# Gated tiles leave PSUM as copies and are split in the last product, and two waits and the opening are set anew, in a two-layer macaron trunk

## The chip, the core and the metric

One Trainium2 chip, one core. The metric is the device time of one execution in microseconds; the kernel before has a median of 2362.59 us over 3 runs (2360.82 to 2363.31).

The engines have their usual short names: PE is TensorE, ACT is ScalarE, DVE is VectorE, POOL is GpSimd and SP is SyncE. A name such as L189 is line 189 of the kernel before. In the changed kernel the lines below the first edit have moved down by up to seven, so L1284 there is L1291, and L915 is L921.

## The reference

The input is one sequence of 512 tokens by 1024 features, and a memory of 256 tokens by 1024. There are two layers; each is a half step of a gated feed-forward net, a mixing step of three gated attention branches, and another half step.

```python
def _swiglu(t, w_gate, w_up, w_down):
    return (jax.nn.silu(t @ w_gate) * (t @ w_up)) @ w_down

for l in range(DEPTH):                                  # DEPTH = 2
    f = _swiglu(_rmsnorm(h, ffn1_pre_g[l]), ffn1_w_gate[l], ffn1_w_up[l], ffn1_w_down[l])
    h = h + 0.5 * _rmsnorm(f, ffn1_post_g[l])
    u = _rmsnorm(h, mix_pre_g[l])
    proj = u @ w_in[l]                                  # q, k, v of two branches, q of the memory branch, forget logits
    o_sb = _stick_breaking_attention(...)               # 8 heads of 64
    o_fx = _forgetting_attention(...)                   # 8 heads of 64
    o_mem = _memory_attention(...)                      # 4 heads of 128
    merged = (g_sb * (_merge_heads(o_sb) @ w_br_sb[l])
              + g_fx * (_merge_heads(o_fx) @ w_br_fox[l])
              + g_mem * (_merge_heads(o_mem) @ w_br_mem[l]))
    h = h + _rmsnorm(merged @ w_out[l], mix_post_g[l])
    f = _swiglu(_rmsnorm(h, ffn2_pre_g[l]), ffn2_w_gate[l], ffn2_w_up[l], ffn2_w_down[l])
    h = h + 0.5 * _rmsnorm(f, ffn2_post_g[l])
```

The hidden width of the feed-forward net is 2816, which is 22 tiles of 128.

## The kernel before

**Products in three passes.** Every factor is kept as two rounded halves, a high and a low one. `split` (L183 to L201) makes them: ACT copies the source into the high half (L188; L191 with a scale), DVE subtracts the high half from the source (L189; L192 with a scale). `mm3` (L214, L215, L216) then issues three matmuls: high by high, high by low, low by high. So each weight tile and each activation needs one ACT copy and one DVE subtraction before PE can finish with it.

**Feed-forward nets.** There are four: a0 and c0 in the first layer, a1 and c1 in the second. Gate and up products run in five groups of four hidden tiles (0, 4, 8, 12 and 16) and two hidden tiles, 20 and 21, that run early. Within a group the product is a block algorithm with seven block products, numbered 0 to 6. ACT and DVE turn the results into the gated tiles, named `ca` in the nets a and `cc` in the nets c. `feature_major` (L777) has PE transpose them into PSUM (tiles `tha`, `thc`). Groups 0 to 12 leave PSUM as plain ACT copies into the `hr` tiles. The last group, 16, leaves PSUM already split, half by half, into the tiles `hid16` and `hid18` (h and l): per net four ACT copies and four DVE subtractions of 128x512.

**The down products.** They are the same block algorithm in 14 steps (`product`), seven products of two halves each, in the order 0, 2, 3, 4, 5, 1, 6. The weights are the `wh_da`/`wl_da` tiles and their sources `bta` and `raw_da`. The other factor is `aa` (`ac` in the nets c): `first_factor` forms a sum or a difference of `hr` tiles into `asa` (L915, L917), and splits it into `aa` by an ACT copy and a DVE subtraction. Hidden tiles 16 to 21 are left out of the block algorithm; `down` multiplies them plainly afterwards, and that is where `hid16` and `hid18` are read. `feature_major` for the last group stands in the schedule beside products 0 and 2.

**Heads.** A stick-breaking head (`stick_head`) computes its scores `zs`, runs a chain of ACT and DVE operations that ends in `ts` (L1315), has PE transpose `ts` block by block into `pts` (`transposed`, L1284), splits those, and multiplies by the values (`pvs`, L1271). A forgetting head does the same with `zf`, `pf` (L1355) and `ptf`. Head (p, j) is head j of pair p.

**What sets the order.** `Q` holds a list of matrix products (gate products `pg`, branch products `pb`, query and key products `pq`, `pk`). `Q.weave` runs a head's chain beside them: a chain step `("wait", t)` says that t us of products are to be issued ahead of the next step. The waits of the stick-breaking heads are `W_SB0` and `W_SB1` plus an entry of the table `W_MORE` (L1414). The framework's scheduler may still issue a single instruction earlier where its own estimate sees PE without work. ACT and DVE serve products and chains from one queue each, in that order.

**The opening.** `begin` (L1715 on) normalises the four 128-token tiles of x; `scaled` writes one half (512 features) of a tile, `turn` transposes it on PE and has ACT copy it out (`us_x`). ACT and DVE run in the written order here (`in_order`). Tiles 2 and 3 are transposed later by `turned` (L613), each behind a wait in us of products.

Of the kernel before, what the change touches and what calls it, by code (L numbers as in the profile page):

```python
# [9 lines left out]
F32 = mybir.dt.float32  # L10
# [7 lines left out]
P = 128  # L18
# [4 lines left out]
def kernel(  # L23
# [38 lines left out]
    nc = tc.nc  # L62
    _, S, D = x.shape
# [41 lines left out]
    def stile(shape, tag, name, dt=F32R):  # L105
        return sb.tile(shape, dt, tag=tag, bufs=BUFS[tag], name=name)
# [4 lines left out]
    def pbank(tag, name):  # L111
        return ps.tile([P, S], F32, tag=tag, bufs=4, name=name)
# [69 lines left out]
    HALVES = (slice(0, S // 2), slice(S // 2, S))  # L182
    FULL = slice(0, S)  # L183

    def split(h_ap, l_ap, src, scale=None, later=False):

        if scale is None:
            both = [nc.scalar.copy(h_ap, src)]  # L188
            make = lambda: nc.vector.tensor_tensor(l_ap, src, h_ap.bitcast(F32), ALU.subtract)  # L189
        else:  # L190
            both = [nc.scalar.activation(h_ap, src, AF.Copy, scale=scale)]  # L191
            make = lambda: nc.vector.scalar_tensor_tensor(l_ap, src, scale, h_ap.bitcast(F32), ALU.mult, ALU.subtract)  # L192
        if later:
            return make
        both.append(make())
        if Q.pinned:
            for ins in both:
                tc.keep_in_program_order(ins)
# [164 lines left out]
    def wpair(src, ktiles, c0, name, scale=None):  # L363

        return [Unit(src, k, min(4, ktiles - k), c0, 256, f"{name}_{k}", scale) for k in range(0, ktiles, 4)]
# [110 lines left out]
    Q = Queue()  # L476
# [8 lines left out]
    def new_h(name):  # L485

        hT[:] = [stile([P, D], "o", f"h{name}_{t}", F32) for t in range(NT)]
# [4 lines left out]
    def rstd(st, a, b=None, pre=None):  # L492

        s, m, y, w = st[:, a:a + 1], st[:, 3:4], st[:, 4:5], st[:, 5:6]
        if pre is not None:
            nc.scalar.activation(y, s, AF.Ln, bias=st[:, pre:pre + 1])
            nc.vector.tensor_scalar(m, s, st[:, pre:pre + 1], None, ALU.add)  # L500
        elif b is None:
            nc.scalar.activation(y, s, AF.Ln, bias=eps_t[:])
            nc.vector.tensor_scalar(m, s, D * EPS, None, ALU.add)
        else:
            nc.vector.tensor_scalar(m, s, st[:, b:b + 1], D * EPS, ALU.add, ALU.add)
            nc.scalar.activation(y, m, AF.Ln)
        nc.scalar.activation(y, y, AF.Exp, scale=-0.5)

        nc.vector.scalar_tensor_tensor(w, m, y, y, ALU.mult, ALU.mult)
        nc.vector.scalar_tensor_tensor(y, w, -3.0, y, ALU.add, ALU.mult)  # L510
        return y

    class Sub:
# [17 lines left out]
        def begin(self):  # L531
            self.fs = [stile([P, D], "f", f"f{self.name}_{t}", F32) for t in range(NT)]
# [100 lines left out]
    TG = (0, 4, 8, 12, 16)  # L633
# [6 lines left out]
    def ffn(l, src, wg, wu, wd, dst, name, spare, aside=None):  # L640
# [5 lines left out]
        hid, st = {}, {}  # L646
        hr = {}
# [14 lines left out]
        def pair(f):  # L662

            i = f // 2
            if i not in hr:
                hr[i] = stile([P, 2, S], HR[i], f"hr{name}_{i}", F32)
            return hr[i]
# [108 lines left out]
        def feature_major(f, of=(0, 1)):  # L776

            for i in of:
                u = st.pop(("hid", f, i))
                for b in range(2):  # L780
                    f2 = f + 2 * b
                    pt = pbank("z", f"th{name}_{f2}_{i}")
                    for m in range(2):
                        for e in range(2):
                            nc.tensor.transpose(pt[:, (2 * m + e) * P:(2 * m + e + 1) * P],
                                                u[:, e, (2 * b + m) * P:(2 * b + m + 1) * P], ident[:])
                    yield 0.45
                    out_ = pt[:].rearrange("p (m q) -> p m q", m=2)
                    if f2 < NC * FC:
                        nc.scalar.copy(pair(f2)[:, :, HALVES[i]], out_)  # L790
                        continue
                    if i == 0:
                        st["hl", b] = [stile([P, 2, S], "v", f"hid{name}_{f2}{x}") for x in "hl"]
                        for m in range(2):
                            hid[f2 + m] = tuple(t[:, m] for t in st["hl", b])
                    split(*(t[:, :, HALVES[i]] for t in st["hl", b]), out_)

        def block_units(order, keep, rows, nm, src, pair=None, c0=0):

# [181 lines left out]
        later = []  # L981
# [6 lines left out]
        def some(n):  # L988
            for one in itertools.islice(todo, n):
                Q.add(*one)  # L990
# [10 lines left out]
        ug, uu = (wpair(w[l], ND, EARLY * P, f"{x}{name}_{EARLY}") for x, w in (("g", wg), ("u", wu)))  # L1001
# [43 lines left out]
        if aside is not None:  # L1045
            Q.add([], lambda: iter((next(norm),)))
            Q.add([], lambda: iter((next(norm),)))
        some(1)
        if aside is not None:
            Q.add([], lambda: norm)  # L1050
# [315 lines left out]
    def mem_head(q, ks, vs, hd, ot, name, begun):  # L1366
# [37 lines left out]
        for kt in range(MT):  # L1404
# [6 lines left out]
    W_SB0, W_SB1 = 12.0, 4.7  # L1411


    W_MORE = {(0, 0): (-8.0, -1.5), (0, 1): (-0.7, -1.0), (1, 0): (0.8, 0.0), (1, 1): (0.5, -1.3),  # L1414
              (2, 0): (-1.0, 0.0), (2, 1): (-0.5, 1.5), (NP - 1, 0): (0.0, 2.5), (NP - 1, 1): (1.0, 0.0)}
    W_FX0, W_FX1 = 6.0, 4.2
    W_MM0, W_MM1 = 6.0, 4.5
# [28 lines left out]
    def mixing(l, src, ks, vs, values, dst):  # L1446
# [187 lines left out]
        def run():  # L1634
# [32 lines left out]
            def stick(p, j):  # L1667
                return stick_head(st["q", 0, p], st["k", 0, p], lambda kt: st["v", 0][kt][:, p], j, st["o", 0][p], f"s{l}_{p}_{j}",
                                  W_MORE.get((p, j), (0.0, 0.0)))

# [43 lines left out]
    def warm(n):  # L1714

        for _ in range(n):
            tc.keep_in_program_order(nc.tensor.matmul(wps[:], wsb[:, 0:P], wsb[:, 0:S], start=True, stop=True))

    def begin():

        sub = subs[0]
        new_h("x")
        Q.hold = True
        nc.sync.dma_start(hT[0][:], x[0, 0:P, :])
        warm(6)
        sub.gains(quick=True)
        nc.sync.dma_start(hT[1][:], x[0, P:2 * P, :])

        ug = Q.jobs[0][0][:4]
        for un in ug[2:]:  # L1730
            un.place = "v"
        for un in ug[:2]:
            un.fetch()
        nc.sync.dma_start(hT[2][:], x[0, 2 * P:3 * P, :])
        for un in ug[2:]:
            un.fetch()
        nc.sync.dma_start(hT[3][:], x[0, 3 * P:4 * P, :])
        sub.begin()
        sub.alloc()
        lows = {}  # L1740

        def turn(t, hf):
            ts_ = slice(t * P, (t + 1) * P)
            pt = pbank("z", f"utx_{t}_{hf}")
            for e in range(4):
                d = 4 * hf + e
                nc.tensor.transpose(pt[:, e * P:(e + 1) * P], sub.fs[t][:, d * P:(d + 1) * P], ident[:])
            lows[t, hf] = split(sub.us[hf][:, :, 0, ts_], sub.us[hf][:, :, 1, ts_],
                                pt[:].rearrange("p (e q) -> p e q", e=4), scale=RS, later=True)

        def stats(t):
            sub.squared(hT[t][:], sub.sh[t], 0, sub.fs[t][:])
            return rstd(sub.sh[t], 0)

        def scaled(t, hf, r):
            nc.vector.scalar_tensor_tensor(sub.fs[t][:, HF[hf]], hT[t][:, HF[hf]], r, sub.spread[hf][:], ALU.mult, ALU.mult)

        with in_order(nc.scalar, nc.vector):
            r = stats(0)
            for hf in range(2):  # L1760
                scaled(0, hf, r)
            r = stats(1)
            warm(2)
            for hf in range(2):
                turn(0, hf)
            low0 = ug[0].split_from(ug[0].raw[:], later=True)
            for hf in range(2):
                scaled(1, hf, r)
            turn(1, 0)
            turn(1, 1)  # L1770
            low1 = ug[1].split_from(ug[1].raw[:], later=True)
            lows[0, 0]()
            lows[1, 0]()
            low0()
            ug[0].loaded()
            lows[0, 1]()
            lows[1, 1]()
            low1()
            ug[1].loaded()
            r = stats(2)  # L1780
            for hf in range(2):
                scaled(2, hf, r)
            for un in ug[2:]:
                un.load()
            for pt, c in zip(sub.spread, HF):
                nc.scalar.copy(sub.gq[:, c], pt[:])
            sub.squared(hT[3][:], sub.sh[3], 0, sub.fs[3][:])
            sub.normed(3)
        sub.done.update((0, 1))
        for t, us_ in ((2, 6.5), (3, 3.2)):  # L1790
            yield ("wait", us_)
            sub.turned(t)
            yield ("pe", 0.9)
# [9 lines left out]
    for l in LAYERS:  # L1803
        i, mn = 3 * l, []
# [42 lines left out]
```

## Time and profile before

| what | value |
|---|---|
| median of 3 runs | 2362.59 us |
| profiled execution, its own time | 2360.91 us |
| its span, first to last instruction | 2359.2 us |
| DVE busy | 1781.2 us (75%) |
| ACT busy | 1445.6 us (61%) |
| POOL busy | 212.5 us (9%) |
| mean granted TensorE clock | 1.000 |

The span is the stretch from the first to the last instruction. The profiled execution's own time is 1.7 us longer, which is what lies around the span, and it is itself 1.7 us below the median of the runs. In a row of the view in order of time stand the start, the length, the engine, the line, the operation with its output and inputs, and the count; a bracket gives the idle time of the engine before the row and what ended it. Matmuls overlap, so the time that a wait costs PE is read from start to start.

### The profile page before, as it was taken

How to read it: one execution, taken by the hardware profiler on the slowest of the kernel's cores; microseconds unless marked ns; L12 is line 12 of the kernel's file. 1: busy time of each engine (PE TensorE's matmuls, PEld its weight loads, DVE VectorE, ACT ScalarE, POOL GpSimd, SP SyncE). 2: the span in 40 equal slices, each digit the busy share in tenths (PEclk: the TensorE clock that was granted, in tenths of full speed). 3: DMA queues.
4: the chain of work that ended last, by engine and by line, in shares of the span. 5: the costliest groups of instructions: out<-in, count | busy, mean ns of one | idle time of the engine just before them, and what ended most of it. 6: DMA issues, size and time to landing. Idle time of an engine off the chain costs nothing.

```text
span 2359.2 us, 30541 instructions
## 1 busy us (share of the span) xinstructions
PE 2346.2 (99%) x11368; PEld 1970.5 (84%) x11368; DVE 1781.2 (75%) x2431; ACT 1445.6 (61%) x2339; POOL 212.5 (9%) x242
## 2 busy tenths in 40 slices
PE   9999999999999999999999999999999999999998
PEld 8888888888888888888888888888888888888887
DVE  8766977678776687769887679766787766866696
ACT  6665665577665565566665566656675555655574
POOL 1101100001020011101011110000011100111100
PEclk9999999999999999999999999999999999999999
DMA  8866854222223476659586767632232234776683
GB/s 246 233 181 173 222 186 144 72 72 81 82 71 116 152 217 175 180 159 245 180 217 172 186 187 222 196 101 81 63 90 81 72 123 154 222 184 173 182 219 99
DMA packets 233112, 366.46 MB, mean 155 GB/s; under 512 B 11242, under 2 KB 101634, under 8 KB 232452
## 3 DMA queue, kind: packets, MB, share of 16 engines
q1 hardware_dynamic: 202400, 305.76, 40.2%
q0 software_dynamic: 30560, 58.76, 14.5%
q8 instruction: 89, 1.46, 0.3%
q14 instruction: 59, 0.48, 0.1%
q10 hardware_dynamic: 4, 0.00, 0.0%
HBM read 349.80 MB, written 14.68 MB: 154 GB/s over the span
## 4 chain that ended last, share of the span: by engine, by line
PE 92%; DVE 5%; issue 1%; ACT 1%; DMA 1%; POOL 0%; SPq 0%; DVEq 0%; POOLq 0%
PE ptc L214 5%; PE ptc L216 5%; PE ptc L215 5%; PE pta L214 5%; PE pta L215 5%; PE pta L216 5%; PE pg L216 3%; PE pg L214 3%; PE pg L215 3%; PE pdc L216 3%; PE pda L216 3%; PE pdc L214 3%; PE pdc L215 3%; PE pda L215 3%; PE pda L214 3%; PE pb L214 2%
## 5 line engine op out<-in xcount | busy, mean ns | idle before, releaser
L214 PE MATMUL pg<-us_a,wh_wg 128*128 128x512 f32 x384 | 151.0, 393 | 0.0
L216 PE MATMUL pg<-us_a,wl_wg 128*128 128x512 f32 x384 | 149.8, 390 | 0.0
L215 PE MATMUL pg<-us_a,wh_wg 128*128 128x512 f32 x384 | 149.7, 390 | 0.0
L189 DVE TENSOR_TENSOR wl_tc<-ktc,wh_tc 128x1024 fp32r<-128x1024 f32 x80 | 97.7, 1224 | 63.3 <-ACT wh_tc L188 63.1
L189 DVE TENSOR_TENSOR wl_ta<-kta,wh_ta 128x1024 fp32r<-128x1024 f32 x80 | 97.7, 1224 | 57.5 <-ACT wh_ta L188 57.5
L188 ACT CAST wh_tc<-ktc 128x1024 fp32r<-128x1024 f32 x80 | 84.0, 1053 | 67.9 <-PE ptc L216 48.0
L214 PE MATMUL pta<-wh_ta,aga 128*128 128x512 f32 x320 | 125.3, 392 | 0.0
L214 PE MATMUL ptc<-wh_tc,agc 128*128 128x512 f32 x320 | 125.3, 393 | 0.0
L216 PE MATMUL pta<-wh_ta,aga 128*128 128x512 f32 x320 | 124.8, 390 | 0.3 <-DVE aga L189 0.3
L216 PE MATMUL ptc<-wh_tc,agc 128*128 128x512 f32 x320 | 124.7, 390 | 0.0
L215 PE MATMUL ptc<-wl_tc,agc 128*128 128x512 f32 x320 | 124.7, 390 | 0.0
L215 PE MATMUL pta<-wl_ta,aga 128*128 128x512 f32 x320 | 124.7, 390 | 0.0
L188 ACT CAST wh_ta<-kta 128x1024 fp32r<-128x1024 f32 x80 | 84.0, 1053 | 65.1 <-PE pta L216 43.6
L189 DVE TENSOR_TENSOR wl_tc<-raw_tc,wh_tc 128x1024 fp32r<-128x1024 f32 x56 | 68.6, 1225 | 45.3 <-ACT wh_tc L188 45.3
L189 DVE TENSOR_TENSOR wl_ta<-raw_ta,wh_ta 128x1024 fp32r<-128x1024 f32 x58 | 70.9, 1224 | 42.2 <-ACT wh_ta L188 42.2
L188 ACT CAST wh_tc<-raw_tc 128x1024 fp32r<-128x1024 f32 x56 | 58.9, 1052 | 48.2 <-PE ptc L216 36.6
L188 ACT CAST wh_ta<-raw_ta 128x1024 fp32r<-128x1024 f32 x58 | 60.8, 1050 | 44.9 <-PE pta L216 37.0
L216 PE MATMUL pdc<-wh_dc,ac 128*128 128x512 f32 x224 | 87.5, 392 | 0.7 <-DVE ac L189 0.7
L216 PE MATMUL pda<-wh_da,aa 128*128 128x512 f32 x224 | 87.4, 392 | 0.7 <-DVE aa L189 0.7
L214 PE MATMUL ptc<-wh_tc,us_b 128*128 128x512 f32 x224 | 87.7, 392 | 0.2
L214 PE MATMUL pda<-wh_da,aa 128*128 128x512 f32 x224 | 87.6, 391 | 0.0
L214 PE MATMUL pdc<-wh_dc,ac 128*128 128x512 f32 x224 | 87.6, 391 | 0.0
(557 smaller groups left out, 7409.8 us busy)
## 6 DMA issues: line engine op xcount, KB each, us to landing
raw_wg<-in_w_gate_dram SPq DMA_DIRECT2D x48, 512.0 KB, 3.7
raw_ta<-in_ffn_w_gate_dram SPq DMA_DIRECT2D x44, 512.0 KB, 4.3
raw_tc<-in_ffn_w_gate_dram SPq DMA_DIRECT2D x44, 512.0 KB, 4.3
raw_da<-in_ffn_w_down_dram SPq DMA_DIRECT2D x42, 512.0 KB, 3.8
raw_dc<-in_ffn_w_down_dram SPq DMA_DIRECT2D x42, 512.0 KB, 3.8
kta<-in_ffn_w_up_dram SPq DMA_DIRECT2D x40, 512.0 KB, 6.5
ktc<-in_ffn_w_up_dram SPq DMA_DIRECT2D x40, 512.0 KB, 5.7
raw_wo<-in_w_out_dram SPq DMA_DIRECT2D x24, 512.0 KB, 3.8
```

Source lines behind the costliest of these rows:

```text
L188: both = [nc.scalar.copy(h_ap, src)]
L189: make = lambda: nc.vector.tensor_tensor(l_ap, src, h_ap.bitcast(F32), ALU.subtract)
L214: nc.tensor.matmul(pt, lh, rh, start=start, stop=False, skip_group_check=free)
L215: nc.tensor.matmul(pt, lh, rl, start=False, stop=False, skip_group_check=free)
L216: nc.tensor.matmul(pt, ll, rh, start=False, stop=stop, skip_group_check=free)
```

## The change

The change has four edits.

1. `feature_major`: the last group's tiles leave PSUM as plain ACT copies into two new tiles `hr..16` and `hr..18`, like those of the other groups. A new function `last_hidden` splits these from SBUF, two ACT copies and two DVE subtractions of 128x1024 per net. It is put ahead of the last product.
2. `W_MORE[(1, 1)]`, the first wait of the stick-breaking head (1, 1), goes from 0.5 to 2.7 on top of `W_SB0`.
3. `begin`: the first halves of tiles 0 and 1 go first, the second halves after; the split of the first weight tile and the two `warm` matmuls change places with transposes.
4. The wait ahead of tile 2's `turned` goes from 6.5 to 8.0.

```diff
@@ feature_major
                     if i == 0:
-                        st["hl", b] = [stile([P, 2, S], "v", f"hid{name}_{f2}{x}") for x in "hl"]
-                        for m in range(2):
-                            hid[f2 + m] = tuple(t[:, m] for t in st["hl", b])
-                    split(*(t[:, :, HALVES[i]] for t in st["hl", b]), out_)
+                        st["last", b] = stile([P, 2, S], "v", f"hr{name}_{f2}", F32)
+                    nc.scalar.copy(st["last", b][:, :, HALVES[i]], out_)
+
+        def last_hidden():
+
+            for b in range(2):
+                both = [stile([P, 2, S], "v", f"hid{name}_{TG[-1] + 2 * b}{x}") for x in "hl"]
+                split(*(t[:] for t in both), st["last", b][:])
+                for m in range(2):
+                    hid[TG[-1] + 2 * b + m] = tuple(t[:, m] for t in both)
@@ the list of work of a net
         if aside is not None:
             Q.add([], lambda: iter((next(norm),)))
             Q.add([], lambda: iter((next(norm),)))
+        Q.add([], lambda: iter(last_hidden() or ()))
         some(1)
@@ the table of waits
-    W_MORE = {(0, 0): (-8.0, -1.5), (0, 1): (-0.7, -1.0), (1, 0): (0.8, 0.0), (1, 1): (0.5, -1.3),
+    W_MORE = {(0, 0): (-8.0, -1.5), (0, 1): (-0.7, -1.0), (1, 0): (0.8, 0.0), (1, 1): (2.7, -1.3),
@@ begin
             r = stats(0)
-            for hf in range(2):
-                scaled(0, hf, r)
-            r = stats(1)
+            scaled(0, 0, r)
+            r1 = stats(1)
+            low0 = ug[0].split_from(ug[0].raw[:], later=True)
+            turn(0, 0)
             warm(2)
-            for hf in range(2):
-                turn(0, hf)
-            low0 = ug[0].split_from(ug[0].raw[:], later=True)
-            for hf in range(2):
-                scaled(1, hf, r)
+            scaled(1, 0, r1)
             turn(1, 0)
-            turn(1, 1)
+            scaled(0, 1, r)
+            scaled(1, 1, r1)
             low1 = ug[1].split_from(ug[1].raw[:], later=True)
+            for t in range(2):
+                turn(t, 1)
...
-        for t, us_ in ((2, 6.5), (3, 3.2)):
+        for t, us_ in ((2, 8.0), (3, 3.2)):
```

**DVE in down product 2 of net a0.** In the names, `hida0_16l` is the low half of hidden tiles 16 and 17, `aa0_0_2` the factor of product 2, `asa0_0_2` and `asa0_1_2` its unsplit sums for the first and the second half, `bta` and `wl_da` weights. Before:

```order
L189 TENSOR_TENSOR hida0_16l_2069<-tha0_16_1_2128,hida0_16h_2068 128x2x256
L189 TENSOR_TENSOR hida0_18l_2078<-tha0_18_1_2135,hida0_18h_2077 128x2x256
L189 TENSOR_TENSOR aa0_0_2_2150<-asa0_0_2_2151,aa0_0_2_2150 128x512
L343 TENSOR_TENSOR bta0_0_0_1937<-bta0_0_0_1937,raw_da0_0_3_0_1977 128x1024
L189 TENSOR_TENSOR wl_da0_1_2_0_2143<-bta0_1_0_1942,wh_da0_1_2_0_2142 128x1024
L343 TENSOR_TENSOR bta0_0_0_1937<-bta0_0_0_1937,raw_da0_0_3_2_1983 128x1024
L189 TENSOR_TENSOR wl_da0_1_2_2_2147<-bta0_1_0_1942,wh_da0_1_2_2_2146 128x1024
L915 TENSOR_TENSOR asa0_1_2_2194<-hra0_6_1829,hra0_4_1529 128x512
L915 TENSOR_TENSOR asa0_1_2_2194<-hra0_7_1836,hra0_5_1536 128x512
L343 TENSOR_TENSOR bta0_1_0_1942<-bta0_1_0_1942,raw_da0_1_3_0_2016 128x1024
L189 TENSOR_TENSOR wl_da0_0_3_0_2186<-bta0_0_0_1937,wh_da0_0_3_0_2185 128x1024
L189 TENSOR_TENSOR aa0_0_2_2150<-asa0_1_2_2194,aa0_0_2_2150 128x512 x2
```

Now, from the same place on (the rows ahead of it are the first half's two sums and a weight's low half):

```order
L921 TENSOR_TENSOR asa0_1_2_2188<-hra0_6_1829,hra0_4_1529 128x512
L189 TENSOR_TENSOR wl_da0_0_2_0_2083<-bta0_0_0_1937,wh_da0_0_2_0_2082 128x1024
L189 TENSOR_TENSOR aa0_0_2_2144<-asa0_0_2_2145,aa0_0_2_2144 128x512 x2
L343 TENSOR_TENSOR bta0_0_0_1937<-bta0_0_0_1937,raw_da0_0_3_0_1977 128x1024
L189 TENSOR_TENSOR wl_da0_0_2_2_2087<-bta0_0_0_1937,wh_da0_0_2_2_2086 128x1024
L189 TENSOR_TENSOR aa0_0_2_2144<-asa0_1_2_2188,aa0_0_2_2144 128x512
L343 TENSOR_TENSOR bta0_0_0_1937<-bta0_0_0_1937,raw_da0_0_3_2_1983 128x1024
L189 TENSOR_TENSOR wl_da0_1_2_0_2137<-bta0_1_0_1942,wh_da0_1_2_0_2136 128x1024
L921 TENSOR_TENSOR asa0_1_2_2188<-hra0_7_1836,hra0_5_1536 128x512
L343 TENSOR_TENSOR bta0_1_0_1942<-bta0_1_0_1942,raw_da0_1_3_0_2016 128x1024
L189 TENSOR_TENSOR wl_da0_1_2_2_2141<-bta0_1_0_1942,wh_da0_1_2_2_2140 128x1024
L189 TENSOR_TENSOR aa0_0_2_2144<-asa0_1_2_2188,aa0_0_2_2144 128x512
```

The two subtractions into `hida0_16l` and `hida0_18l` are gone from here, and the first low part that is made from `asa0_1_2`, in the last row of the first listing, is in the sixth row of the second. The subtractions into `hida0_16l` and `hida0_18l` now stand in product 6, between the weights `wl_da0_0_6_2` and `wl_da0_1_6_0`. On ACT the copy into `hida0_16h` stays in product 2, right after the copies out of PSUM; the copy into `hida0_18h` is in product 6.

**PE at head (1, 1) of the first layer.** `pb0_2_3` is a branch product, `pq0_0_3` a query product that runs beside the head, `pts0_1_1_0` the head's first bank of transposes. Before:

```order
L216 MATMUL pb0_2_3_4511<-om0_3_3386,wl_wb0_2_1_0_4096 128x512
L1284 MATMUL pts0_1_1_0_4540<-ident_65,ts0_1_1_1_4451 128x128
L214 MATMUL pq0_0_3_4525<-us_a0_0_3053,wh_q0_0_3_4299 128x512
...
L216 MATMUL pq0_0_3_4525<-us_a0_0_3053,wl_q0_0_3_4300 128x512
L1284 MATMUL pts0_1_1_0_4540<-ident_65,ts0_1_1_1_4451 128x128
L1284 MATMUL pts0_1_1_0_4540<-ident_65,ts0_1_1_2_4439 128x128
L1284 MATMUL pts0_1_1_0_4540<-ident_65,ts0_1_1_3_4429 128x128
L1284 MATMUL pts0_1_1_1_4547<-ident_65,ts0_1_1_1_4451 128x128
```

Now:

```order
L216 MATMUL pb0_2_3_4513<-om0_3_3388,wl_wb0_2_1_0_4098 128x512
L1291 MATMUL pts0_1_1_0_4551<-ident_65,ts0_1_1_1_4453 128x128
L214 MATMUL pq0_0_3_4527<-us_a0_0_3055,wh_q0_0_3_4301 128x512
...
L216 MATMUL pq0_0_3_4527<-us_a0_1_3056,wl_q0_0_3_4302 128x512
L1291 MATMUL pts0_1_1_0_4551<-ident_65,ts0_1_1_1_4453 128x128
L1291 MATMUL pts0_1_1_0_4551<-ident_65,ts0_1_1_2_4441 128x128
L1291 MATMUL pts0_1_1_0_4551<-ident_65,ts0_1_1_3_4431 128x128
L1291 MATMUL pts0_1_1_1_4558<-ident_65,ts0_1_1_1_4453 128x128
```

The rows left out are matmuls of `pq0_0_3`: 12 of them stood between the first transpose and the other nine, and now 21 do. The first transpose has kept its place, right behind the last matmul of `pb0_2_3`. Everything of this chain and of the later ones stands nine or ten matmuls later beside the products. On DVE the low half of the weight `wl_v0_1_0_4` has thereby moved ahead of the softmax chain of the forgetting head (2, 0), of which `pf0_2_0_0` is the last tile; it stood inside this chain.

**DVE between the first two groups of net a0.** `mem_rstd` and `mraw` belong to the normalisation of the memory, `wl_ta0_4_0_0` is the first weight of group 4, `ca` gated tiles. Before:

```order
L771 TENSOR_SCALAR ca0_0_01_688<-ca0_0_01_688,ca0_0_00_409 128x1024
L189 TENSOR_TENSOR wl_ta0_0_6_2_700<-kta0_0_0_2_230,wh_ta0_0_6_2_699 128x1024
L1165 TENSOR_TENSOR mem_rstd_81<-mem_rstd_81 128x2
L1166 TENSOR_SCALAR mem_rstd_81<-mem_rstd_81 128x2
L1167 TENSOR_TENSOR mem_rstd_81<-mem_rstd_81 128x2
L1185 TENSOR_SCALAR mraw0_0_2652<-mraw0_0_2652,mem_rstd_81 128x1024
L189 TENSOR_TENSOR wl_ta0_4_0_0_739<-raw_ta0_4_0_0_613,wh_ta0_4_0_0_738 128x1024
L764 TENSOR_TENSOR ca0_0_11_653<-ca0_0_11_653,pta0_0_0_0_383 128x512
L764 TENSOR_TENSOR ca0_0_11_653<-ca0_0_11_653,pta0_0_0_1_384 128x512
```

Now:

```order
L189 TENSOR_TENSOR wl_ta0_0_6_2_700<-kta0_0_0_2_230,wh_ta0_0_6_2_699 128x1024
L771 TENSOR_SCALAR ca0_0_01_688<-ca0_0_01_688,ca0_0_00_409 128x1024
L189 TENSOR_TENSOR wl_ta0_4_0_0_739<-raw_ta0_4_0_0_613,wh_ta0_4_0_0_738 128x1024
L764 TENSOR_TENSOR ca0_0_11_653<-ca0_0_11_653,pta0_0_0_0_349 128x512
L764 TENSOR_TENSOR ca0_0_11_653<-ca0_0_11_653,pta0_0_0_1_350 128x512
L1168 TENSOR_SCALAR mem_rstd_81<-mem_rstd_81 128x2
L189 TENSOR_TENSOR wl_ta0_4_0_2_745<-raw_ta0_4_0_2_619,wh_ta0_4_0_2_744 128x1024
L1171 TENSOR_TENSOR mem_rstd_81<-mem_rstd_81 128x2
L1172 TENSOR_TENSOR mem_rstd_81<-mem_rstd_81 128x2
L1173 TENSOR_SCALAR mem_rstd_81<-mem_rstd_81 128x2
L1174 TENSOR_TENSOR mem_rstd_81<-mem_rstd_81 128x2
L1192 TENSOR_SCALAR mraw0_0_2646<-mraw0_0_2646,mem_rstd_81 128x1024
```

The small operations on `mem_rstd` and the scaling of `mraw0_0` stood ahead of `wl_ta0_4_0_0`; now they come behind it.

At the opening PE issues the transposes of tile 0's first half, the two `warm` matmuls, tile 1's first half, and then the two second halves; all 16 transposes still come ahead of the first product `pga`. The transposes of tile 3 stand six matmuls later. On SP a few loads and stores change places with their neighbours.

## The prediction

> **What bounds the kernel now.** I read the page of the profile first, for the shares.
>
> ```profile
> PE 2346.2 (99%) x11368; PEld 1970.5 (84%) x11368; DVE 1781.2 (75%) x2431; ACT 1445.6 (61%) x2339; POOL 212.5 (9%) x242
> ```
>
> PE is busy in all but 13 us of the 2359.2 us span. The change removes no matmul and adds none, so it can gain only what PE waits for, and lose by making it wait. The next view is that of the waits, for PE alone.
>
> ```profile
> PE pts L1284 <- ACT ts L1315: 1.5, 2, 0.7
> PE pdc L216 <- DVE ac L189: 0.7, 2, 0.3
> PE pda L216 <- DVE aa L189: 0.7, 2, 0.3
> PE ptf L1284 <- DVE pf L1355: 0.4, 2, 0.2
> ...
> PE utx L613 <- DVE fx L603: 0.3, 1, 0.3
> PE pta L216 <- DVE aga L189: 0.3, 1, 0.3
> PE pta L215 <- DVE wl_ta L189: 0.2, 1, 0.2
> ```
>
> Each row is one place per layer (or one at the start): who waited for whom, the total, the count, the longest. Matmul ends overlap the next start, so these figures are too small; the true price is read from start to start in the view in order of time. There is little to win: a handful of waits, each under 1.3 us, and each edit stands beside one of them.
>
> **Part 1, the last group's split.** The place is down product 2, here of net a0.
>
> ```profile
> 256.21 0.39 PE L214 MATMUL pda<-wh_da,aa 128*128 128x512 f32 x1
> 256.44 0.39 PE L215 MATMUL pda<-wl_da,aa 128*128 128x512 f32 x1
> 257.17 0.74 PE L216 MATMUL pda<-wh_da,aa 128*128 128x512 f32 x2 [0.34 <-DVE aa L189]
> ```
>
> Matmuls start 0.23 us apart. The third comes 0.73 us after the second, 0.50 too late, and the row of two takes 0.74 where 0.39 + 0.23 = 0.62 is usual, 0.12 more as PE takes up its pace again. So the wait costs 0.62 us, and the waits view counts it once in each of the four nets. DVE, beside it:
>
> ```profile
> 246.61 0.69 DVE L189 TENSOR_TENSOR hida_16l<-tha,hida_16h 128x512 fp32r<-128x512 f32 x1
> ...
> 247.81 0.69 DVE L189 TENSOR_TENSOR aa<-asa,aa 128x512 fp32r<-128x512 f32 x1
> 248.41 1.23 DVE L343 TENSOR_TENSOR bta<-bta,raw_da 128x1024 f32<-128x1024 f32 x1
> ...
> 256.42 1.30 DVE L189 TENSOR_TENSOR aa<-asa,aa 128x512 fp32r<-128x512 f32 x2
> ```
>
> The low part that PE waits for is the first of the pair at 256.42. It is late because the queue is full: four subtractions into `hid16` and `hid18` stand ahead of it, and the second half's sums come last. In the new order the same low part stands where the second low part stood (247.81). Ahead of it four subtractions of 0.69 (2.76 us) have gone, and one sum and one low part of 128x512 and one weight sum of 128x1024 have come (0.69 + 0.69 + 1.23 = 2.61 us). It ends by about 248.5, eight microseconds before PE wants it. The wait goes: **4 x 0.62 = 2.5 us gained**. I looked for what is late next: the other low part of the second half now stands three weight operations of 1.23 and a sum later, near 254, still ahead of 257. So I take the full 2.5; the least is nothing, if another weight is late by as much.
>
> What the edit adds comes later. It splits from SBUF in pieces of 128x1024, priced by the page's groups:
>
> ```profile
> L189 DVE TENSOR_TENSOR wl_ta<-kta,wh_ta 128x1024 fp32r<-128x1024 f32 x80 | 97.7, 1224 | 57.5 <-ACT wh_ta L188 57.5
> ...
> L188 ACT CAST wh_ta<-kta 128x1024 fp32r<-128x1024 f32 x80 | 84.0, 1053 | 65.1 <-PE pta L216 43.6
> ```
>
> Per net ACT has 2 x 1.05 = 2.1 us more (its four copies out of PSUM stay), and DVE 2 x 1.22 = 2.45 us in product 6 for 4 x 0.69 = 2.76 us in product 2. The cover in product 6:
>
> ```profile
> 303.16 1.05 ACT L188 CAST wh_da<-bta 128x1024 fp32r<-128x1024 f32 x1 [1.66 <-PE pda L216]
> 304.31 1.23 DVE L189 TENSOR_TENSOR wl_da<-bta,wh_da 128x1024 fp32r<-128x1024 f32 x1
> ...
> 311.08 0.39 PE L214 MATMUL pda<-wh_da,aa 128*128 128x512 f32 x1
> ...
> 317.75 0.48 PE L214 MATMUL pda<-wh_da,hida_16h 128*128 128x512 f32 x1
> ```
>
> The two subtractions stand just ahead of the weight low part at 304.31. It ended at 305.54 and its first product began at 311.08, so there are 5.5 us of cover for 2.45. ACT had 1.66 us free ahead of 303.16 for the one copy of 1.05 that falls there; the other copy stays in product 2. The hidden tiles themselves are read from 317.75 on. I cost this at nothing. Without the cover the price is 4 x 2.45 = 9.8 us on DVE or 4 x 2.1 = 8.4 us on ACT.
>
> The Trainium skill (VectorE: DVE Perf Modes, section "Rules for kernel authors") advises reading a matmul's output straight from PSUM unless many operations follow, and copying it out first only then. Here two operations follow, so by that rule the extra copies are a loss: with ACT setting the pace they would turn the sum of this prediction from a gain of 3.8 us into a loss of 4.6. The trace speaks against it at this place, since ACT idles 1.66 us there; it is one form of the uncovered split among the rivals.
>
> **Part 2, head (1, 1).** The wait that it stands beside is the largest:
>
> ```profile
> 513.70 0.51 ACT L1315 ACTIVATE ts<-ts 128x384 f32<-128x384 f32 x1
> 513.82 0.75 DVE L209 SCALAR_TENSOR_TENSOR ga<-pg,nbgate,ga 128x512 f32<-128x512 f32 x1
> ...
> 513.12 0.39 PE L216 MATMUL pb<-om,wl_wb 128*128 128x512 f32 x1
> 514.25 0.33 PE L1284 MATMUL pts<-ident,ts 128*128 128x128 f32 x1 [0.74 <-ACT ts L1315]
> 514.63 0.50 PE L214 MATMUL pq<-us_a,wh_q 128*128 128x512 f32 x1
> ```
>
> From 513.12 to 514.25 are 1.13 us, 0.90 above the pace, and PE then starts the product 0.38 us later; about 0.15 would do for one small transpose. That is about 1.1 us in each layer. A later chain would cure it, but the new order moves nine of the ten transposes and leaves the first where it was, right behind the product `pb`. PE still waits there for `ts`, which ends at 514.21. Even with that transpose gone, `pq` would wait for the gate product's bank, which DVE frees at 513.82 + 0.75 = 514.57. **Nothing gained here**; at most 2 x 1.1 = 2.2 us if the bound were only the transpose.
>
> The side effect is that all later chains of the mixing step run nine matmuls (9 x 0.23 = 2.1 us) later beside the products. One wait is touched for the better, the forgetting head (2, 0):
>
> ```profile
> 620.50 1.22 DVE L189 TENSOR_TENSOR wl_v<-raw_v,wh_v 128x1024 fp32r<-128x1024 f32 x1
> ...
> 624.34 0.39 PE L216 MATMUL pb<-o,wl_wb 128*128 128x512 f32 x1
> ...
> 624.50 0.29 DVE L1355 TENSOR_SCALAR pf<-pf,stf 128x128 f32<-128x128 f32 x1
> ...
> 624.93 0.74 PE L1284 MATMUL ptf<-ident,pf 128*128 128x128 f32 x5 [0.20 <-DVE pf L1355]
> ```
>
> PE starts the transposes 0.59 us after the last product matmul, 0.36 late, because the last `pf` ends at 624.79. The weight's low part at 620.50, 1.22 us long, now comes ahead of this chain, so `pf` should end about a microsecond earlier: **2 x 0.36 = 0.7 us gained**, at least nothing. The other chains now meet other neighbours; a new wait of the size of the old one in any of them costs up to 2 x 1.1 us.
>
> **Parts 3 and 4, the opening.** By halves the second product starts sooner, since the weight copy can use an idle stretch of ACT, and tile 3's transposes, 0.3 us late by the waits view, get six matmuls more.
>
> ```profile
> 9.62 0.60 ACT L191 ACTIVATE us_x<-utx 128x512 fp32r<-128x512 f32 x1 [1.70 <-PE utx L1747]
> ...
> 13.98 0.74 PE L849 MATMUL pga<-us_x,w_ga 128*128 128x256 f32 x4 [0.21 <-ACT w_ga L188]
> ...
> 31.20:61.10 29.90, 29.66 (x176) 26.18 (x175) 29.25 (x37) 21.58 (x28) 5.09 (x5) 1.00 0.79 194
> ...
> 59.87 2.36 DVE L189 TENSOR_TENSOR aga<-ra,aga 128x1024 fp32r<-128x1024 f32 x2
> ...
> 61.15 0.50 PE L216 MATMUL pta<-wh_ta,aga 128*128 128x512 f32 x1 [0.29 <-DVE aga L189]
> ```
>
> The weight copy of 1.05 us fits into the 1.70, but the second half's `us_x` copies come behind it, so I put the lead at 0.1 us, and with the 0.3 to 0.5 of tile 3 at 0.4 to 0.6. It does not last. From 31.2 to 61.1 the third of the busy figures, DVE's, is 29.25 of 29.90 us: DVE has no room, the work ahead of `aga` in its queue is the same as before, and at 61.15 PE waits for just that. A PE that comes there earlier waits longer. **Net 0**, up to 0.6 gained.
>
> Behind that place one wait does change:
>
> ```profile
> 70.94 0.75 DVE L1185 TENSOR_SCALAR mraw<-mraw,mem_rstd 128x1024 f32<-128x1024 f32 x1
> 71.61 1.22 DVE L189 TENSOR_TENSOR wl_ta<-raw_ta,wh_ta 128x1024 fp32r<-128x1024 f32 x1
> ...
> 72.14 0.49 PE L214 MATMUL pta<-wh_ta,us_x 128*128 128x512 f32 x1
> 72.88 0.50 PE L215 MATMUL pta<-wl_ta,us_x 128*128 128x512 f32 x1 [0.24 <-DVE wl_ta L189]
> ```
>
> PE starts 0.74 us after the matmul before, 0.51 late, and that row is 0.11 longer than the usual 0.39. The weight's low part at 71.61 now stands ahead of `mraw` and the small operations before it, so it ends at least 0.75 us earlier: **0.6 us gained**, at least nothing.
>
> **Sum.** 2.5 + 0.7 + 0.6 = 3.8 us. The profiled execution took 2360.91 us, so it would take 2357.1; it is 1.7 below the median of the runs, 2362.59, which goes to 2358.8.
>
> **The rivals.** *The gain is given back.* A wait that goes brings PE to the next weight earlier, and where DVE is full, as from 31 to 61, that weight is then late. In the down products DVE was late by 0.62 with a full queue. If half the 2.5 returns and the two smaller gains do not hold, 1.2 stay: 2361.4. For it: DVE is busy without a break around 248. Against: the new low part has eight microseconds to spare. *More goes than counted.* Head (1, 1) loses its wait as well, because the products around it shift: 3.8 + 2.2 = 6.0, so 2356.6. Against it stands the unmoved first transpose. *The late split is not covered.* ACT or DVE reaches product 6 later than before, the two subtractions hold up the weight behind them, and 2.45 us per net reach PE: 9.8 - 3.8 = 6.0 slower, 2368.6. It decides once DVE reaches that place more than 5.5 - 2.45 = 3.1 us later than now. *New waits in later heads*: each costs 2.2 us in two layers, so two of them undo the sum and give 2363.2. *Nothing*: the four low parts turn out to be released by something else, and the time stays at 2362.6; I count this with the first rival.
>
> **How the numbers follow.** The forecast has 0.47, the gain given back (or nothing) 0.25, more than counted 0.14, the uncovered split 0.08, new waits 0.06. The predicted time is 2358.8. A measurement of this kernel tells some 0.2%, 4.7 us, from no change, so faster means below 2357.9 and slower above 2367.3. The forecast lies just inside; its own range, 2356.8 to 2360.8, puts 0.4 of it beyond. Faster: 0.4 x 0.47 + 0.14 = 0.33. Slower: most of the uncovered split and a little of the new waits, 0.09. The same: 0.58. The range that holds 8 in 10 reaches down past 2356.6 to 2355, and up past 2363.2 to 2364.5; the uncovered split stays outside.
>
> **What would show it.** Right: the rows `pda <- aa` and `pdc <- ac` leave PE's waits, as do `ptf <- pf` and `wl_ta`; `pts <- ts` stays at 1.5 in two; the row for `aga` grows. Product 6 shows no PE idle. Wrong would be PE idle in front of `wl_da` or a `hid` tile in product 6, waits of 0.5 us and more at new heads, or `pts <- ts` gone.

## The result, and the profile after

The changed kernel has a median of 2365.4 us over 22 runs (2363.71 to 2366.75); the kernel before, run beside it, 2360.78 us over 22 (2359.22 to 2364.98). The medians differ by 4.6 us, to the slower side, where 3.8 us faster was forecast. The ratio of the runs is 1.0017 (4.0 us), 95% interval 1.001 to 1.0024. The profiled execution of the changed kernel took 2366.39 us, its span is 2364.4 us, 5.2 more than before.

The first line of its page, and the waits of PE (who waited for whom, total, times, longest):

```profile
PE 2347.8 (99%) x11368; PEld 1973.8 (83%) x11368; DVE 1780.5 (75%) x2423; ACT 1452.1 (61%) x2347; POOL 213.2 (9%) x242
```

```profile
PE pts L1291 <- ACT ts L1322: 7.0, 4, 2.8
PE warm L1724 <- DVE warm L1808: 1.3, 1, 1.3
PE pta L216 <- DVE aga L189: 1.2, 1, 1.2
```

Of the seven rows that the prediction showed of this view five are gone: `pda <- aa`, `pdc <- ac`, `ptf <- pf`, `utx <- fx` and `wl_ta`. The row `pts <- ts` has grown from 1.5 us in two places to 7.0 in four. PE also has 1.6 us more busy time for the same number of matmuls, so some matmuls ran slower. Both stand at one place, here in the first layer, in the view in order of time of PE:

```profile
582.76 0.39 PE L216 MATMUL pg<-us_a,wl_wg 128*128 128x512 f32 x1
585.90 1.31 PE L1291 MATMUL pts<-ident,ts 128*128 128x128 f32 x10 [2.75 <-ACT ts L1322]
586.97 0.50 PE L214 MATMUL pg<-us_a,wh_wg 128*128 128x512 f32 x1
587.28 0.61 PE L215 MATMUL pg<-us_a,wh_wg 128*128 128x512 f32 x1
587.69 0.63 PE L216 MATMUL pg<-us_a,wl_wg 128*128 128x512 f32 x1
...
590.67 0.41 PE L214 MATMUL pg<-us_a,wh_wg 128*128 128x512 f32 x1
```

These are the transposes of stick-breaking head (3, 0), the first of the last pair. They start 3.14 us after the matmul before, 2.9 late. Behind them eight matmuls take 590.67 - 587.28 = 3.39 us, where 8 x 0.227 = 1.82 is the pace: 1.57 us more. The second layer repeats it at 1756.87, with 2.9 and 1.7 us. The view by stretches has the granted clock in the third figure from the end:

```profile
583.00:586.00 3.00, 0.25 (x2) 0.11 (x2) 2.59 (x5) 1.18 (x3) 0.72 (x2) 1.00 0.00 0
586.00:588.00 2.00, 2.00 (x13) 1.86 (x14) 1.32 (x2) 2.00 (x4) 0.00 (x0) 0.82 0.00 0
588.00:590.00 2.00, 2.00 (x6) 1.51 (x6) 2.00 (x5) 1.21 (x4) 0.00 (x0) 0.50 0.16 13
590.00:591.00 1.00, 1.00 (x5) 0.77 (x4) 0.25 (x2) 0.00 (x0) 0.00 (x0) 0.65 0.83 210
```

PE is idle until 585.9, and after that the clock is down to half of full speed for some 3.4 us: the shortfalls 2 x 0.18, 2 x 0.50 and 1 x 0.35 add up to 1.71, twice which is 3.4. Why head (3, 0) is late is to be read on DVE. First the changed kernel, then the kernel before, in order of time:

```profile
569.85 0.74 DVE L1443 SCALAR_TENSOR_TENSOR fa<-pfl,nbfor,fa 8x512 f32<-8x512 f32 x1 [0.54 <-ACT fa L1442]
...
571.34 1.21 DVE L1444 TENSOR_TENSOR_SCAN fb<-bfor,fa 8x512 f32<-8x512 f32 x1
...
573.31 1.11 DVE L1448 TENSOR_TENSOR cs<-fb,cs 8x512 fp32r<-8x512 f32 x1
...
575.17 1.25 DVE L1339 TENSOR_SCALAR qk<-cs,sel 64x512 fp32r<-64x512 f32 x2
576.45 0.69 DVE L1313 SCALAR_TENSOR_TENSOR ts<-zs,ts 128x512 f32<-128x512 f32 x1
...
584.73 0.56 DVE L1321 TENSOR_TENSOR ts<-zs,ts 128x384 f32<-128x384 f32 x1
```

```profile
571.13 0.69 DVE L1306 SCALAR_TENSOR_TENSOR ts<-zs,ts 128x512 f32<-128x512 f32 x1
...
578.70 0.56 DVE L1314 TENSOR_TENSOR ts<-zs,ts 128x384 f32<-128x384 f32 x1
...
581.15 0.74 DVE L1436 SCALAR_TENSOR_TENSOR fa<-pfl,nbfor,fa 8x512 f32<-8x512 f32 x1
...
582.41 1.20 DVE L1437 TENSOR_TENSOR_SCAN fb<-bfor,fa 8x512 f32<-8x512 f32 x1
...
584.37 0.87 DVE L1441 TENSOR_TENSOR cs<-fb,cs 8x512 fp32r<-8x512 f32 x1
```

`fa`, `fb` and `cs` are the cumulative sum of the forget gate, a job in the list of products; `qk` prepares the first forgetting heads from it. Before, the head's chain (first to last `ts`) ran ahead of it. Now the chain comes nine matmuls later beside the products, and the job has kept its place there. On PE its transposes `pfl` stand just ahead of the pair's key product in both kernels: before at 570.09, behind the head's scores `zs` at 567.41, and now at 566.32, ahead of `zs` at 568.75. So 0.74 + 1.21 + 1.11 + 1.25 = 4.3 us of DVE work now stand ahead of the first `ts`.

The 5.2 us of the spans, from the start-to-start times of PE in both traces:

| place | us |
|---|---|
| waits at head (3, 0), 2 x 2.91 | +5.8 |
| matmuls at half clock behind them, 1.6 + 1.7 | +3.3 |
| forgetting heads: old wait gone (2 x 0.37), a new one (2 x 0.21) | -0.3 |
| waits of the four down products, with the small ones behind them | -3.2 |
| opening, up to 90 us | -0.3 |
| sum of these | +5.3 |
| left over, rounding of the rows | -0.1 |

### The profile page after: what moved, and what is told of

Same layout as the page of the kernel before. It is cut to its first block, busy times and chain, and to the rows that moved or that the text cites. A ratio compares the mean times of both kernels' runs of the same rounds, so it can differ in the third digit from the quotient of the medians.

```text
span 2364.4 us, 30557 instructions
## 1 busy us (share of the span) xinstructions
PE 2347.8 (99%) x11368; PEld 1973.8 (83%) x11368; DVE 1780.5 (75%) x2423; ACT 1452.1 (61%) x2347; POOL 213.2 (9%) x242
## 4 chain that ended last, share of the span: by engine, by line
PE 94%; DVE 2%; ACT 1%; issue 0%; DMA 0%; POOL 0%; DVEq 0%; SPq 0%; ACTq 0%; POOLq 0%
PE ptc L214 5%; PE ptc L216 5%; PE ptc L215 5%; PE pta L214 5%; PE pta L216 5%; PE pta L215 5%; PE pg L215 3%; PE pg L214 3%; PE pg L216 3%; PE pdc L216 3%; PE pdc L214 3%; PE pda L215 3%; PE pdc L215 3%; PE pda L216 3%; PE pda L214 3%; PE pb L215 2%
## 5 line engine op out<-in xcount | busy, mean ns | idle before, releaser
L214 PE MATMUL ptc<-wh_tc,us_b 128*128 128x512 f32 x224 | 87.7, 392 | 0.2
L214 PE MATMUL pda<-wh_da,aa 128*128 128x512 f32 x224 | 87.6, 391 | 0.0
L216 PE MATMUL ptc<-wh_tc,us_b 128*128 128x512 f32 x224 | 87.3, 390 | 0.0
```

What stands on the lines that cost most here:

```text
L214: nc.tensor.matmul(pt, lh, rh, start=start, stop=False, skip_group_check=free)
L216: nc.tensor.matmul(pt, ll, rh, start=False, stop=stop, skip_group_check=free)
```

## The experiments

All ran beside the kernel before. "Span" is that of the profiled execution; before it is 2359.2 us.

| experiment | median, us (runs) | before, median | ratio, 95% interval | span |
|---|---|---|---|---|
| no shift | 2356.46 (11) | 2360.48 | 0.9982, 0.9973 to 0.9991 | 2354.8 |
| shift only | 2367.24 (8) | 2360.48 | 1.0029, 1.0019 to 1.0039 | 2364.0 |
| copies only | 2356.54 (11) | 2360.48 | 0.9982, 0.9973 to 0.9991 | 2355.7 |
| opening only | 2360.76 (11) | 2360.48 | 1.0002, 0.9993 to 1.0011 | 2358.4 |
| filler | 2362.66 (11) | 2360.61 | 1.0008, 0.9999 to 1.0017 | 2360.8 |
| repaid | 2359.72 (11) | 2360.61 | 0.9995, 0.9987 to 1.0004 | 2358.4 |
| early chain | 2353.15 (5) | 2360.61 | 0.9967, 0.9954 to 0.9979 | 2351.1 |
| head (3, 0) later | 2356.17 (11) | 2360.61 | 0.9979, 0.9970 to 0.9988 | 2354.0 |
| gate later | 2356.54 (11) | 2360.71 | 0.9981, 0.9972 to 0.9990 | 2354.5 |

**Which edit.** Four kernels take the change apart.

No shift, the changed kernel with one number back:

```diff
-    W_MORE = {..., (1, 1): (2.7, -1.3),
+    W_MORE = {..., (1, 1): (0.5, -1.3),
```

> The changed kernel with head (1,1)'s wait back at 0.5. Theory A (the later chains put the forget gate's work ahead of head (3,0) on DVE, PE idles there 2.9 us in each layer and the clock falls behind it): the two long waits go, the granted clock is 1.000 again, and the span is 2364.4 - 2 x 2.9 - 2 x 1.6 (slow matmuls) + 0.3 (the forgetting heads) = 2355.7 us, 3.5 below the kernel before. Theory B (the late split or the opening holds PE up): the span stays at or above 2359. Theory C (A's wait, but the fall of the clock comes from something else in the change): span 2358.5 or so, clock still below 1.

The waits of PE in its trace:

```profile
PE pts L1291 <- ACT ts L1322: 1.5, 2, 0.7
PE pta L216 <- DVE aga L189: 1.3, 1, 1.3
PE warm L1724 <- DVE warm L1808: 1.3, 1, 1.3
PE ptf L1291 <- DVE pf L1362: 0.4, 2, 0.2
```

The long waits are gone, the wait of head (1, 1) is what it was in both kernels, and that of forgetting head (2, 0) is back. The span is 2354.8, 0.9 below what theory A said, and theories B and C fall. Against the changed kernel the median is 8.9 us lower: so much does this one number cost there.

Shift only, the same number in the kernel before:

```diff
-    W_MORE = {..., (1, 1): (0.5, -1.3),
+    W_MORE = {..., (1, 1): (2.7, -1.3),
```

> The kernel before with head (1,1)'s wait at 2.7 and nothing else. Theory A: PE waits 2.9 us at head (3,0) in each layer, the granted clock falls to 0.998, the span is 2359.2 + 5.8 + 3.2 - 0.3 = 2367.9 us, 8.7 longer, ratio 1.0037. Theory B: within 1 us of 2359.2.

The median is 6.8 us longer, the span of the profiled execution 4.8, where 8.7 was expected. This execution's opening was 1.5 us shorter than that of the kernel before. The two waits at head (3, 0) are there, of 2.91 us each, but in this execution the clock held behind them:

```profile
582.39 0.39 PE L216 MATMUL pg<-us_a,wl_wg 128*128 128x512 f32 x1
585.53 1.31 PE L1284 MATMUL pts<-ident,ts 128*128 128x128 f32 x10 [2.75 <-ACT ts L1315]
586.60 0.48 PE L214 MATMUL pg<-us_a,wh_wg 128*128 128x512 f32 x1
586.91 0.40 PE L215 MATMUL pg<-us_a,wh_wg 128*128 128x512 f32 x1
587.15 0.40 PE L216 MATMUL pg<-us_a,wl_wg 128*128 128x512 f32 x1
```

So a gap of this length does not always bring the clock down. This execution (2365.9 us) is among the faster of its eight, which reach 2370.13; that the slower ones paid for the clock is likely but was not seen.

Copies only and opening only are the first edit alone, and the third with the wait of 8.0 alone, in the kernel before, as in the diff of the change.

> The kernel before with the last group's copies and late split alone. Theory A: the waits of the four down products go (4 x 0.62, and some 0.1 at each a little later) and nothing comes for them, span 2356.3 to 2356.7 us, ratio 0.9988. Theory B: not below 2359, with PE idle in product 6 or 1.

> The kernel before with the new opening and the wait of 8.0 alone. Theory A: a lead of about 1 us at 61 us is given back to the wait for aga, of which 0.3 to 0.5 us stays behind 73 us: span 2358.7 to 2358.9 us, not to be told from the kernel before. Theory B: longer than 2360.

The copies gain 3.9 us in the median (3.5 in the span), more than the 2.5 to 2.9 expected, and every wait of the down products goes. The opening gains nothing that can be told, as theory A has it, though its median is 0.3 above the kernel before and not below.

**The clock.** Filler puts PE to work in the gap; the result is unchanged, since the transposes overwrite the bank.

```diff
             pt = pbank("z", f"pt{name}_{kt}")
+            if kt == 0 and name[0] == "s" and name.endswith("_3_0"):
+                for _ in range(12):
+                    nc.tensor.matmul(pt[:], ident16, begins16[:], start=True, stop=True, skip_group_check=True)
```

> The changed kernel with twelve matmuls of 512 columns on constants (2.7 us) put ahead of head (3,0)'s transposes, into their bank, which they overwrite. They fill most of the 2.9 us in which PE waits and change nothing else. If the fall of the clock follows from PE's idleness, the transposes start as before, the matmuls behind them keep the pace of 0.23 us, and 2 x 1.6 us go: median 2362.2 us, granted clock 0.999 or 1.000. If the clock falls for another reason, nothing changes: 2365.4 us and 0.998. If the fillers are themselves held up, it is longer.

In order of time on PE (one of the twelve has no record):

```profile
583.03 2.54 PE L1292 MATMUL pts<-begins,ident 128*128 128x512 bf16 x11
585.72 1.31 PE L1294 MATMUL pts<-ident,ts 128*128 128x128 f32 x10 [0.15 <-ACT ts L1325]
586.79 0.48 PE L214 MATMUL pg<-us_a,wh_wg 128*128 128x512 f32 x1
587.11 0.39 PE L215 MATMUL pg<-us_a,wh_wg 128*128 128x512 f32 x1
```

The transposes come no sooner, and the matmuls behind them keep the pace of 0.23 us. The median falls from 2365.4 to 2362.66 us, 2.7 of the expected 3.2. So that much of the loss is the clock after the idle time, and it goes though the wait stays.

**The cause of the wait.** Three kernels keep head (1, 1)'s wait at 2.7 and change one other thing: head (2, 0)'s first wait from -1.0 to -3.2 (repaid), head (3, 0)'s from 0.0 to 3.5 (head (3, 0) later), and the place of the forget gate's job (gate later).

> The changed kernel with head (2,0)'s first wait 2.2 shorter (-3.2 for -1.0), so that head (1,1)'s transposes stay late and the chains behind it return to their places. Theory A (the loss is head (3,0) falling behind the forget gate's work on DVE): the two waits of 2.9 us and the fall of the clock go, span 2355 us, median 2356.5, the 0.4 at the forgetting heads comes back. Rival (the late transposes of head (1,1) cost by themselves): 2358 or more.

> The changed kernel with head (3,0)'s first wait 3.5 longer. The forget gate's work stays ahead of this head on DVE. If it is only that the head's result is 2.9 us late for its place on PE, the wait and the fall of the clock go and nothing else changes: span 2364.4 - 5.8 - 3.2 = 2355.4 us, median 2357. If DVE itself is the bound there, the wait comes back elsewhere: 2361 or more.

```diff
-                if (br, p, x) == (1, FOX[0], "q"):
+                if (br, p, x) == (1, FOX[0], "k"):
                     Q.add([], lambda: forget_cumsum(l, st["fl"], st))
```

> The changed kernel, all chains as late as in it, with the forget gate's job moved from ahead of the key product of its pair to behind it, so that its DVE operations come after head (3,0)'s chain. Theory A in its narrow form (it is these operations, about 4 us on DVE, that make the head late): the two waits of 2.9 us and the fall of the clock go, span 2364.4 - 5.8 - 3.2 = 2355.4 us, median 2357. Rival (the later chains meet a full DVE whatever stands there): PE still waits over 1.5 us at this head, 2360 or more.

Gate later settles it: with every chain as late as in the changed kernel and only this job moved, the span is 2354.5 and `pts <- ts` is down to the old two places:

```profile
PE pta L216 <- DVE aga L189: 1.5, 1, 1.5
PE pts L1291 <- ACT ts L1322: 1.5, 2, 0.7
```

On DVE the head's chain now starts at 572.73, where it started at 576.45 in the changed kernel, and the job comes behind most of it:

```profile
572.73 0.69 DVE L1313 SCALAR_TENSOR_TENSOR ts<-zs,ts 128x512 f32<-128x512 f32 x1 [0.96 <-ACT ts L1312]
...
580.44 0.71 DVE L1443 SCALAR_TENSOR_TENSOR fa<-pfl,nbfor,fa 8x512 f32<-8x512 f32 x1
```

Head (3, 0) later comes out at the same time (2354.0) with the job still ahead of the head: DVE is not full there, the head was only late for its place. Repaid missed its number by 3.2 us, and by the number it lies with the rival (2358 or more), by which the late transposes of head (1, 1) cost by themselves. The trace and gate later, which keeps them as late and has 2354.5, speak against the rival. The waits at head (3, 0) went, as theory A says, and head (2, 0) got one in their stead, 1.58 us above the pace in each layer, because its scores still come behind the later head (1, 1) and only its transposes went back:

```profile
535.53 0.39 PE L215 MATMUL pg<-us_a,wh_wg 128*128 128x512 f32 x1
537.34 1.31 PE L1291 MATMUL pts<-ident,ts 128*128 128x128 f32 x10 [1.42 <-ACT ts L1322]
538.41 0.48 PE L216 MATMUL pg<-us_a,wl_wg 128*128 128x512 f32 x1
538.73 0.39 PE L214 MATMUL pg<-us_a,wh_wg 128*128 128x512 f32 x1
```

Behind this 1.6 us of idle time the clock column stays at 1.00, and from 538.73 on the matmuls start 0.23 us apart. The 0.32 ahead of that is what stands behind such transposes elsewhere (0.31 from 586.60 to 586.91 in shift only).

**A version that beats both.** Early chain leaves the shift out and starts head (1, 1)'s scores 1.5 us sooner, with its transposes at their old place:

```diff
-    W_MORE = {..., (1, 0): (0.8, 0.0), (1, 1): (2.7, -1.3),
+    W_MORE = {..., (1, 0): (0.8, -1.5), (1, 1): (2.0, -1.3),
```

> The changed kernel without the shift, and head (1,1)'s scores 1.5 us earlier (second wait of head (1,0) 0.0 to -1.5) with its transposes where they were (0.5 to 2.0). If the old wait of 1.17 us at these transposes is the chain's own lateness, it goes in both layers: span 2354.8 - 2.3 = 2352.5 us, median 2354.1. If the bank that the gate product holds (DVE ends with it 0.3 us after the chain) sets it as much, less than 0.6 us goes: median 2355.9 or more.

```profile
PE utx L1754 <- ACT nhx L502: 1.6, 1, 1.6
PE warm L1724 <- DVE warm L1808: 1.3, 1, 1.3
PE pta L216 <- DVE aga L189: 1.1, 1, 1.1
PE pga L855 <- ACT us_x L191: 0.4, 1, 0.4
```

After 73 us PE waits for nothing that this view lists. The time is 2353.15 us, 7.5 below the kernel before beside it. The wait of 1.17 us at head (1, 1) went with the chain's lateness: `ts` ends at 508.78 and `ga`, which frees the bank, at 509.87, both ahead of the first `pq` at 511.24, and the stray first transpose goes back to the others. Since both came sooner, this run does not tell which of the two held PE before. The span is 1.4 us below the expected 2352.5. The wait at forgetting head (2, 0) went as well (0.7), which was not expected, and this execution's opening was 0.4 shorter than that of no shift; that leaves 0.3.

## Why the prediction was wrong

*The down products* (2.5 us): right in mechanism, and under-sized. The low part was forecast to end by about 248.5, and does so at 247.98:

```profile
247.29 0.69 DVE L189 TENSOR_TENSOR aa<-asa,aa 128x512 fp32r<-128x512 f32 x1
```

Alone the edit is worth 3.9 us in the median, 3.5 in the span. From start to start the four places of copies only give 3.5, 0.84 to 0.92 each. The sum took 0.62: it left out a second small gap of 0.17 us some 8 us later (rows of 265.10 and 265.44 in net a0 before), and about 0.1 by which the matmuls behind both gaps come a little slower. In the changed kernel the four give 3.2. The reading of "three weight operations" ahead of the other low part is wrong too, since four stand there; it ended at 253.73, still in time.

*The late split at no cost*: right. The two subtractions stand where the order said:

```profile
301.40 1.24 DVE L189 TENSOR_TENSOR hida_16l<-hra,hida_16h 128x1024 fp32r<-128x1024 f32 x1
302.54 1.24 DVE L189 TENSOR_TENSOR hida_18l<-hra,hida_18h 128x1024 fp32r<-128x1024 f32 x1
303.67 1.24 DVE L189 TENSOR_TENSOR wl_da<-bta,wh_da 128x1024 fp32r<-128x1024 f32 x1
```

The weight behind them ends at 304.91, before anything waits for it. The rule of the Trainium skill that the prediction cites (VectorE: DVE Perf Modes, section "Rules for kernel authors") has the copy out of PSUM first only for many operations. Two follow here, and the copy paid all the same: copies only gained 3.9 us.

*Head (1, 1) gains nothing*: right, its wait stayed at 1.17 us in both layers. But "even with that transpose gone, `pq` would wait for the gate product's bank" held only for this order; early chain moved both.

*The side effect of the shift* is the step that failed. The prediction put it at a gain of 0.7 us at forgetting head (2, 0) and said of the rest that "a new wait of the size of the old one in any of them costs up to 2 x 1.1 us", with 0.06 for the rival of new waits. The gain came, less 0.2 us per layer at another forgetting head. But the bound was taken from the old wait, which says nothing of a new one's size: that is set by what a chain is moved past. Here that was a job that does not move with the chains, 4.3 us of DVE work against 2.0 us of delay, and PE lost 2.9 us per layer. The rival of new waits had 2.2 us for such a place in two layers; with the half clock behind it this one cost 9.1 (5.8 and 3.3). In the order of the changed kernel `fb`, `cs` and `qk` stand ahead of head (3, 0)'s `ts` instead of behind, and the prediction has no term for that place. Its own sign of being wrong, waits of 0.5 us and more at new heads, is what came. Without the shift the other edits give 4.0 us in the median (no shift), where the sum had 3.1.

*No price for what follows an idle PE.* The sum counted a wait at its length. The half clock behind it cost 3.3 us more in this execution, and 2.7 in the median by the filler.

*The opening, net 0*: right. PE came to that place 0.8 us ahead, and gave the lead back at 61 us, where it now starts at 61.33 for 61.15 before:

```profile
61.33 0.50 PE L216 MATMUL pta<-wh_ta,aga 128*128 128x512 f32 x1 [1.24 <-DVE aga L189]
```

*The first weight of group 4* (0.6 us): its wait went. The matmul starts 0.33 us after the one before it (72.36 to 72.69), where it took 0.74. By opening only nothing of it can be told in the median.

## What to carry to other kernels

When a wait in a chain is lengthened, follow every later chain of that sequence past the jobs that stay in place, engine by engine, and price the work that changes sides; the waits that exist today do not bound it. An idle stretch of PE near 3 us cost half as much again behind it here (1.6 us for 2.9), so break it up or fill it before trimming shorter ones. Starting the late chain sooner gained what giving it more time could not.

## What the runs showed of the hardware

A wait of 1.6 us left the clock alone (repaid); 2.9 us of it brought the clock to half for 3.4 us in both layers of one execution, and in neither of another with the same waits (shift only). The Trainium skill (TensorE: Matmul & The Clock Gate, Part 1) describes a gate that watches a free-running window of about 3.4 us. The 3.4 us at half clock agree with that, and so does its coming in one execution and not in the other; the window itself no run here shows directly. The Trainium skill warns in the same page's section "Why this matters for your kernels" of idle gaps over about 3 us. Here 2.9 us were enough.

Idle time alone does not settle it. In the opening of shift only the column, third from the end, falls to 0.59 between 8 and 12 us, though PE's last wait ahead of that is only 1.05 us (to 7.77). The eight transposes from 7.77 take 1.87 us there, where eight such at 18.09 take 1.03.

```profile
8.00:12.00 4.00, 3.66 (x18) 3.04 (x17) 2.99 (x8) 2.93 (x5) 0.24 (x1) 0.59 1.07 367
```

What else counts there was not tested.

In the first microseconds the clock column can't be relied on. The four matmuls `gqx` took 3.78 us in the kernel before and 2.19 in shift only, which has the same opening, while the column gives 1.00 for the slower one. The rows of `gqx` come first, before and shift only, then the stretch of the kernel before:

```profile
3.99 3.78 PE L545 MATMUL gqx<-grow,ones 1*128 1x512 f32 x4
```

```profile
3.99 2.19 PE L545 MATMUL gqx<-grow,ones 1*128 1x512 f32 x4
```

```profile
4.00:7.70 3.70, 3.70 (x5) 1.16 (x5) 1.28 (x4) 2.98 (x7) 0.53 (x2) 1.00 1.06 382
```

So the same opening takes a different time in these two executions (the transposes of tile 3 start at 25.98 us in the first and at 25.18 in the second), and edits there can't be judged by one profile.
